# One more step of rest at three places of a two-layer attention and convolution trunk

## The chip, the core and the metric

The kernel runs on one core of one Trainium2 chip. The metric is the device time of one execution, in microseconds (us). Five engines work side by side, each through its own queue in order: TensorE (PE) does the matrix products, with its weight loads shown apart as PEld; VectorE (DVE) and ScalarE (ACT) work elementwise; GpSimd (POOL) does a little arithmetic and issues accumulating DMAs; SyncE (SP) issues the other DMAs. They wait for each other by semaphores.

## What is computed

Two layers run over 256 latent tokens of width 1024, with 256 context tokens beside them (512 columns in layer 0, 256 in layer 1, where only the latent tokens go on after the keys and values). The half of a layer that the change touches, cut to what matters:

```python
h = modulate(rmsnorm(x, norm1_g[l]), sh1, sc1)
p = h @ w_in[l]                                  # GLU, q, k, v, gates
u = dwconv1d(a * sigmoid(g), dw, dw_b)           # 31 taps, 512 channels
u = silu(layernorm(u, ln_g, ln_b))
y_conv = u @ w_conv_out[l]
y_attn = merge_heads(neighbourhood_attention(q, k, v, k_c, v_c, rpb)) @ w_na_out[l]
g_conv, g_attn = split(sigmoid(p[..., QKV_END:]))
x = x + g1 * ((g_conv * y_conv + g_attn * y_attn) @ w_out[l])
```

The second half of a layer is a gated MLP (2816 wide) with a convolution of width 3. A last RMSNorm gives the output. The modulation (shifts, scales and gates of both halves) is computed from a conditioning vector and six 1024 x 1024 matrices a layer.

## The kernel before

**Products.** Everything is float32. A weight tile is split into a high part `whi` and a low part `wlo`, an activation likewise, and each product is three matmuls: high by high (L197), high by low of the activation (L198), low of the weight by high (L199). A group is one block of 128 output channels: 8 tiles of weights, 24 matmuls, where the depth is 1024, and 4 tiles, 12 matmuls, where it is 512. The moving side has 512 columns in layer 0 and 256 in layer 1.

**Weights.** They come from memory in units of 512 KB (128 x 1024 floats) into a ring of four raw buffers; `whi` and `wlo` have four buffers each. A plain unit (`wunit`) is cast on ACT (L167), and DVE subtracts for the low part (L168). A unit in the set `ADDED` (`wadded`) goes another way: ACT casts (L216) and writes minus the high part (L217), and POOL issues a DMA that adds the raw unit onto it (L218). The cast into a `whi` buffer waits until PE has read what lay there, four units ago. In layer 0 the second and fourth unit of the attention's projection (NA) and all four of the convolution's projection (CO) are in `ADDED`.

**Side work.** Generators run beside the groups. `slot()` steps each of them once: after every group of 256 columns, and twice, in the middle and at the end, in a group of 512 columns. What a generator emits in a step lands in the program at that place; the scheduler that builds the program then sets each engine's order, by the data's ties and by its own estimate of the time. Such generators are: the attention's scores and values (`Attention.step`), the 31 taps of the convolution (L673), the modulation's dot products on DVE (`ada_dots`, L304, with rows `own` loaded by SP), and the layer norm of the convolution's branch.

**The layer norm** (`layer_norm`, L938) does, with yields between: the last taps; the sum over the four channel tiles (L951); a matmul with ones for the mean, L955, into the bank "po"; the subtraction of the mean (L958) and the sums of squares (squares L345 and L352 on ACT, sums L356 on DVE); the matmul that sums the squares, L370; the root on DVE and POOL (L378, L380); the transposes that spread it, L386; then for each tile j the scaling (L966), swish on ACT (L967), its high part `sh` (L968) and low part `sl` (L969). `last` is the second layer. After the gate groups come the eight NA groups (their result is multiplied onto a gate at L993 on DVE, which frees the bank), then the eight CO groups, which read `sh` and `sl`; their result is worked up at L998 to L1001 into `z`, named `h` in the trace, for the output projection.

**The attention** (`Attention.step`, L457): `n` counts steps, `at` is the step of its last action, `todo` holds pairs of heads with the step at which they came in.

Of the kernel before, what the change touches and what calls it, by code (L numbers as in the profile page):

```python
# [53 lines left out]
def trunk(ctx: ExitStack, tc: tile.TileContext, xt, cvec, crow, wall, wada, params, bias_t, rope_t, out):  # L54
# [13 lines left out]
    def nm(s):  # L68
        uid[0] += 1
        return f"{s}_{uid[0]}"  # L70
# [3 lines left out]
    def psum(tag="main"):  # L74
        return psp.tile([P, 512], F32, tag=tag, bufs=BANKS[tag], name=nm(tag))

    def tmp(w=512):
        return tp.tile([P, w], F32, tag="t", bufs=5, name=nm("t"))
# [67 lines left out]
    def pr(l, off, n):  # L146
        return par[:, l * NPAR + off : l * NPAR + off + n]
# [211 lines left out]
    def sum_squares(n, T, apart=False):  # L359

        at = tp.tile([P, 512], F32, tag="ss", name=nm("ss"))
        return [SumSq(T, at[:, i * T : (i + 1) * T], apart) for i in range(n)]

    def rstd(ss, n, bank, rest=0):

        nt = ss.T // P
        pt = psum("pt")
        for i, p in enumerate(ss.parts):
            for t in range(nt):
                pe.matmul(  # L370
                    pt[:, t : t + 1], sl(p, t), one, start=i == 0 and t == 0, stop=i == len(ss.parts) - 1,
                    skip_group_check=True,
                )
        return (yield from root(pt, nt, n, bank, rest))
# [48 lines left out]
    class Attention:  # L423
# [33 lines left out]
        def step(self, now=False):  # L457
            self.n += 1
            since = self.n - self.at
            alone = self.soft and not self.pv and not self.late  # L460
            rest = 4 if self.todo or alone else 3 if self.soft else 2
            if not now and since < (3 if alone and self.l else rest) and not self.late:
                return
            if not now and not alone and not self.todo and self.pairs < 4:
                return
            if not now and not alone and self.todo and self.n - self.todo[0][0] < 2:
                return
            if self.late:
                if not self.todo or self.n - self.todo[0][0] < 2:
                    return  # L470
                self.late, self.at = False, self.n
                return self.issue()
            if alone and not now:
                self.late = True
            self.at = self.n
            pv, self.pv = self.pv, []
            soft, self.soft = self.soft, []
            for what, its, pps in soft:
                with tc.issue_after(self.last.ins), tc.issue_after(self.done.ins):
                    self.turn(what, its, pps)  # L480
            for work in pv:
                self.values(*work, "sc" if work[0] == CTX and not (soft or self.todo) else "po")
            if self.todo and not self.late:
                self.issue()
# [147 lines left out]
    for l in range(DEPTH):  # L632
        last = l == DEPTH - 1
# [4 lines left out]
        with ExitStack() if last else start as e1a:  # L638
# [21 lines left out]
            def conv_tap(j, t):  # L660
                if after[0] is not None:
                    with tc.issue_after(after[0].ins):
                        tap(j, t)
                else:
                    tap(j, t)
# [259 lines left out]
            with ExitStack() as e1c:  # L925
# [12 lines left out]
                def layer_norm():  # L938

                    while taps:  # L940
                        for _ in range(6 if last else 5):
                            if taps:
                                conv_tap(*taps.pop(0))
                        yield
                    pace[0] = 1.0 if last else 1.2
                    flat = [c.rearrange("p s t -> p (s t)") for c in cb]
                    sm = tp.tile([P, 512], F32, tag="ss", name=nm("ss"))
                    eng = pool if last else dve
                    eng.tensor_tensor(sm[:, :T], flat[0], flat[1], ALU.add)
                    eng.tensor_tensor(sm[:, :T], sm[:, :T], flat[2], ALU.add)  # L950
                    dve.tensor_tensor(sm[:, :T], sm[:, :T], flat[3], ALU.add)  # L951
                    for _ in range(1 if last else 5):
                        yield
                    pm = psum("po")
                    pe.matmul(pm[:, :T], one.to_broadcast([P, P]), sm[:, :T], start=True, stop=True)  # L955
                    (s2,) = sum_squares(1, T)
                    for j in range(KC):
                        dve.scalar_tensor_tensor(flat[j], pm[:, :T], -1.0 / CONV, flat[j], ALU.mult, ALU.add)  # L958
                        s2.add(flat[j], j == KC - 1)
                    for _ in range(2 if last else 5):  # L960
                        yield
                    pb = yield from rstd(s2, CONV, "po", 0 if last else 2)
                    for j in range(KC):
                        sg = tmp()
                        g, b = pr(l, LNG + j, 1), pr(l, LNB + j, 1)
                        dve.scalar_tensor_tensor(flat[j], flat[j], g, pb[:, :T], ALU.mult, ALU.mult)  # L966
                        act.activation(sg[:, :T], flat[j], AF.Silu, bias=b)  # L967
                        act.copy(sh_[j], sg[:, :T])  # L968
                        dve.tensor_tensor(sl_[j], sg[:, :T], sh_[j].bitcast(F32), ALU.subtract)  # L969
                        yield  # L970
                    if last:
                        pace[0] = 0.4

                side.remove(conv)
                ln = layer_norm()
                add_side(ln)
                for n in range(n, 2 * KD):
# [356 lines left out]
```

## Time and profile before

| | us |
|---|---|
| median of 3 runs | 1056.72 (1055.75 to 1057.86) |
| the profiled execution, whole | 1057.85 |
| its span on the engines | 1056.0 |
| mean clock granted to TensorE | 0.996 of full speed |
| DVE busy in L168 | 252.5 (211 instructions) |
| DVE busy in L304 | 151.4 (120) |
| ACT busy in L167 | 217.6 (211) |

The page of the profile gives busy times by engine, groups of instructions by line, the chain of work that ended last, and DMA queues. A row of the timeline has the start, the duration, the engine, the line, the operation, output and inputs, and in brackets the idle time of its engine just before it and what ended that. PE rows overlap: matmuls are pipelined, so the pace is the distance of starts. DMA transfers are timed from issue to landing.

### The profile page before, as it was taken

Reading aid. Unit: us, or ns where it says so; the run is one execution under the profiler, and the core shown is the slowest. Engines: PE = TensorE matmul, PEld = TensorE weight load, DVE = VectorE, ACT = ScalarE, POOL = GpSimd, SP = SyncE. Lnnn points to the kernel's source line nnn. Section 1 sums busy time; section 2 is a strip of 40 time slices with the busy share of each in tenths; the row PEclk is TensorE's granted clock in tenths of the full one; section 3 lists DMA queues with packets and bytes.
Section 4 is the critical chain, followed back from the end, with each engine's and each line's share of the span. In section 5 each row is a group of like instructions: output and inputs, shape, how many; then the busy total and the mean of one; then the engine's idle time right before and its main releaser. Section 6 shows DMA issues by size and latency. Waiting matters only on the chain.

```text
span 1056.0 us, 18062 instructions
## 1 busy us (share of the span) xinstructions
PE 1033.4 (98%) x6886; PEld 933.1 (88%) x6886; DVE 892.1 (84%) x1630; ACT 568.1 (54%) x943; POOL 43.5 (4%) x59
## 2 busy tenths in 40 slices
PE   9999999999999999999999999999999999999997
PEld 7787788888889988888888889999889999999996
DVE  6568899999998788888889887799999988898883
ACT  4458868545434644444444223545776666667652
POOL 1111110011000000000000000000000000000000
PEclk9999999999999999999999999999999999999998
DMA  9988674888945345454545887556744484676781
GB/s 376 304 226 214 150 183 129 246 264 236 304 146 179 101 140 160 140 163 149 165 141 159 302 285 252 180 184 213 211 130 130 163 284 143 193 217 187 227 290 59
DMA packets 59511, 209.26 MB, mean 198 GB/s; under 512 B 7200, under 2 KB 7456, under 8 KB 59424
## 3 DMA queue, kind: packets, MB, share of 16 engines
q1 hardware_dynamic: 54384, 190.77, 55.6%
q0 software_dynamic: 4752, 17.30, 8.6%
q8 instruction: 54, 0.88, 0.3%
q14 instruction: 33, 0.27, 0.1%
q10 hardware_dynamic: 288, 0.04, 0.0%
HBM read 187.63 MB, written 1.05 MB: 179 GB/s over the span
## 4 chain that ended last, share of the span: by engine, by line
PE 68%; DVE 18%; ACT 5%; DMA 4%; issue 3%; SPq 1%; DVEq 0%; ACTq 0%
PE main L197 20%; PE main L198 20%; PE main L199 19%; DVE cb L673 6%; PE main L736 4%; DMA raw<-in_wall 3%; DVE wlo L168 2%; DVE t L304 2%; SPq L728 1%; PE sc L197 1%; PE sc L198 1%; PE sc L199 1%; ACT whi L167 1%; DVE qk L882 1%; PE po L230 1%
## 5 line engine op out<-in xcount | busy, mean ns | idle before, releaser
L197 PE MATMUL main<-h,whi 128*128 128x256 f32 (+1 forms) x1328 | 433.5, 327 | 1.9 <-DVE qk L882 1.2
L199 PE MATMUL main<-h,wlo 128*128 128x256 f32 (+1 forms) x1328 | 430.0, 325 | 3.0 <-DVE wlo L168 2.9
L198 PE MATMUL main<-h,whi 128*128 128x256 f32 (+1 forms) x1328 | 430.4, 325 | 0.9 <-DVE h L1001 0.7
L167 ACT CAST whi<-raw 128x1024 fp32r<-128x1024 f32 (+1 forms) x211 | 217.6, 1036 | 216.1 <-PE main L198 166.6
L168 DVE TENSOR_TENSOR wlo<-raw,whi 128x1024 fp32r<-128x1024 f32 (+1 forms) x211 | 252.5, 1203 | 66.4 <-ACT whi L167 66.0
L197 PEld LDWEIGHTS main<-h,whi 128*128 128x128 f32 x1328 | 253.0, 191 | 23.4 <-issue 1.7
L199 PEld LDWEIGHTS main<-h,wlo 128*128 128x128 f32 x1328 | 252.5, 191 | 20.6 <-DVE wlo L168 3.7
L198 PEld LDWEIGHTS main<-h,whi 128*128 128x128 f32 x1328 | 253.0, 191 | 18.3 <-DVE h L1001 1.0
L304 DVE CUSTOM_DVE_ANT_0 t<-own,sb,par 128x1024 bf16<-128x1024 f32 x120 | 151.4, 1277 | 7.2 <-DMA own<-in_wada 7.1
L673 DVE SCALAR_TENSOR_TENSOR cb<-u,par,cb 128x512 f32<-128x512 f32 (+1 forms) x240 | 144.1, 615 | 2.8
L198 PE MATMUL main<-fl,whi 128*128 128x256 f32 (+1 forms) x396 | 122.7, 310 | 0.0
L197 PE MATMUL main<-fh,whi 128*128 128x256 f32 (+1 forms) x396 | 122.7, 310 | 0.0
L199 PE MATMUL main<-fh,wlo 128*128 128x256 f32 (+1 forms) x396 | 122.6, 310 | 0.0
L198 PEld LDWEIGHTS main<-fl,whi 128*128 128x128 f32 x396 | 75.6, 191 | 3.6
L199 PEld LDWEIGHTS main<-fh,wlo 128*128 128x128 f32 x396 | 75.6, 191 | 3.5
L197 PEld LDWEIGHTS main<-fh,whi 128*128 128x128 f32 x396 | 75.6, 191 | 3.5
L216 ACT CAST whi<-raw 128x1024 fp32r<-128x1024 f32 x33 | 34.6, 1048 | 36.7 <-PE main L198 30.0
L1070 ACT ACTIVATE t<-main,par 128x512 f32<-128x512 f32 (+1 forms) x82 | 50.6, 666 | 0.7 <-PE main L199 0.7
L1071 DVE SCALAR_TENSOR_TENSOR t<-main,par,t 128x510 f32<-128x510 f32 (+1 forms) x82 | 47.3, 612 | 1.1 <-ACT t L1070 0.8
L1074 DVE SCALAR_TENSOR_TENSOR t<-main,par,t 128x510 f32<-128x510 f32 (+1 forms) x82 | 46.7, 609 | 0.0
L1083 ACT ACTIVATE t<-t 128x512 f32<-128x512 f32 (+1 forms) x44 | 23.1, 524 | 43.4 <-DVE t L1074 42.9
L404 ACT ACTIVATE h<-t,mod 128x256 fp32r<-128x256 f32 x56 | 25.2, 501 | 35.1 <-DVE t L403 34.7
(207 smaller groups left out, 1217.3 us busy)
## 6 DMA issues: line engine op xcount, KB each, us to landing
raw<-in_wall SPq DMA_DIRECT2D x240, 512.0 KB, 4.4
own<-in_wada SPq DMA_DIRECT2D x72, 512.0 KB, 4.7
wlo<-raw POOLq DMA_DIRECT2D x33, 512.0 KB, 5.5
raw<-in_wada SPq DMA_DIRECT2D x16, 512.0 KB, 5.9
bias<-in_bias_t SPq DMA_DIRECT2D x8, 520.0 KB, 5.1
row<-in_wada SPq DMA_DIRECT2D x8, 512.0 KB, 5.1
sb<-in_crow SPq DMA_DIRECT2D x5, 512.0 KB, 4.7
x<-in_xt SPq DMA_DIRECT2D x4, 512.0 KB, 5.0
```

Source lines behind the costliest of these rows:

```text
L167: act.copy(hi[:, c], r[:, c])
L168: dve.tensor_tensor(lo[:, c], r[:, c], hi[:, c].bitcast(F32), ALU.subtract)
L197: pe.matmul(ps, w[0], order(xh), start=start, stop=False)
L198: pe.matmul(ps, w[0], order(xl), start=False, stop=False)
L199: pe.matmul(ps, w[1], order(xh), start=False, stop=stop)
L216: act.copy(hi, r)
L304: dve.tensor_tensor_reduce(tmp().bitcast(BF16), r, v, 1.0, pr(l, BADA + n, 1), ALU.mult, ALU.add, mods[l][:, n, s : s + 1])
L673: dve.scalar_tensor_tensor(cb[j], src, w, cb[j], ALU.mult, ALU.add)
L736: mm = pe.matmul(pv[t], h1[n == 1][k][:, c], runs(w[n == 2][:, b]), start=k + n == 0, stop=k == KD - 1 and n == 2)
L1070: act.activation(c, pv_, AF.Identity, bias=pr(l, FDB + t, 1), scale=w[1])
L1071: dve.scalar_tensor_tensor(c[:, :, 1:], pv_[:, :, : S - 1], w[0], c[:, :, 1:], ALU.mult, ALU.add)
L1074: dve.scalar_tensor_tensor(c[:, :, : S - 1], pv_[:, :, 1:], w[2], c[:, :, : S - 1], ALU.mult, ALU.add)
```

## The change

Three numbers. The attention's first scores ask for three steps since the first pair came in instead of two, as long as no action has been taken (`at` is 0); layer 0's layer norm yields six times instead of five between the sum of the channel tiles and the mean's matmul; layer 1's yields three times instead of two between the sums of squares and the matmul that adds them up.

```diff
--- before.py
+++ after.py
@@ -463,7 +463,7 @@
                 return
             if not now and not alone and not self.todo and self.pairs < 4:
                 return
-            if not now and not alone and self.todo and self.n - self.todo[0][0] < 2:
+            if not now and not alone and self.todo and self.n - self.todo[0][0] < (2 if self.at else 3):
                 return
             if self.late:
                 if not self.todo or self.n - self.todo[0][0] < 2:
@@ -949,7 +949,7 @@
                     eng.tensor_tensor(sm[:, :T], flat[0], flat[1], ALU.add)
                     eng.tensor_tensor(sm[:, :T], sm[:, :T], flat[2], ALU.add)
                     dve.tensor_tensor(sm[:, :T], sm[:, :T], flat[3], ALU.add)
-                    for _ in range(1 if last else 5):
+                    for _ in range(1 if last else 6):
                         yield
                     pm = psum("po")
                     pe.matmul(pm[:, :T], one.to_broadcast([P, P]), sm[:, :T], start=True, stop=True)
@@ -957,7 +957,7 @@
                     for j in range(KC):
                         dve.scalar_tensor_tensor(flat[j], pm[:, :T], -1.0 / CONV, flat[j], ALU.mult, ALU.add)
                         s2.add(flat[j], j == KC - 1)
-                    for _ in range(2 if last else 5):
+                    for _ in range(3 if last else 5):
                         yield
                     pb = yield from rstd(s2, CONV, "po", 0 if last else 2)
                     for j in range(KC):
```

The first place leaves the order of instructions on every engine as it is. The others move instructions on PE, DVE and ACT, and on SP and POOL the loads and accumulates tied to them. In layer 0 L955, L370 and L386 stand 12 matmuls later on PE. DVE has two more of the modulation's dot products (L304) ahead of the sum L951.

First place, ACT in layer 0, from the cast of NA's fourth unit (`whi_2814`, low part `wlo_2815`) on; 2855 and 2904 are the casts of CO's first two units, and g_15 the last gate. Before:

```order
L216 CAST whi_2814<-raw_2812 128x1024
L711 ACTIVATE g_15_2667<-main_2614 128x512
L217 ACTIVATE wlo_2815<-whi_2814 128x1024
L967 ACTIVATE t_2662<-cb_3_187,par 128x512
L968 CAST sh_3_2152<-t_2662 128x512
L216 CAST whi_2855<-raw_2853 128x1024
L217 ACTIVATE wlo_2856<-whi_2855 128x1024
L216 CAST whi_2904<-raw_2902 128x1024
L217 ACTIVATE wlo_2905<-whi_2904 128x1024
```

After:

```order
L216 CAST whi_2814<-raw_2812 128x1024
L711 ACTIVATE g_15_2662<-main_2609 128x512
L967 ACTIVATE t_2657<-cb_2_186,par 128x512
L968 CAST sh_2_2151<-t_2657 128x512
L967 ACTIVATE t_2693<-cb_3_187,par 128x512
L968 CAST sh_3_2152<-t_2693 128x512
L216 CAST whi_2855<-raw_2853 128x1024
L216 CAST whi_2904<-raw_2902 128x1024
L217 ACTIVATE wlo_2815<-whi_2814 128x1024
L217 ACTIVATE wlo_2856<-whi_2855 128x1024
L217 ACTIVATE wlo_2905<-whi_2904 128x1024
```

The negated copy L217 into `wlo_2815` moved behind the swish of tiles 2 and 3 and behind the casts `whi_2855` and `whi_2904`.

Second place, DVE in layer 0, around the low part of NA's third unit, `wlo_2768`; g_8 to g_11 are the gates that NA's groups 0 to 3 are multiplied onto, `own` rows feed L304 (its second row reads out the accumulator). Before:

```order
L969 TENSOR_TENSOR sl_2_2155<-t_2639,sh_2_2151 128x512
L304 ISA t_2658,mod_105<-own_2583,sb_2146,par 128x1024
L304 ISA mod_105 128x1
L966 SCALAR_TENSOR_TENSOR cb_3_187<-cb_3_187,par,po_2585 128x512
L168 TENSOR_TENSOR wlo_2768<-raw_2766,whi_2767 128x1024
L304 ISA t_2712,mod_105<-own_2637,sb_2143,par 128x1024
L304 ISA mod_105 128x1
L969 TENSOR_TENSOR sl_3_2156<-t_2662,sh_3_2152 128x512
L993 SCALAR_TENSOR_TENSOR g_8_2328<-g_8_2328,main_2691 128x512
```

After:

```order
L993 SCALAR_TENSOR_TENSOR g_9_2367<-g_9_2367,main_2705 128x512
L304 ISA t_2745,mod_105<-own_2655,sb_2143,par 128x1024
L304 ISA mod_105 128x1
L304 ISA t_2747,mod_105<-own_2655,sb_2146,par 128x1024
L304 ISA mod_105 128x1
L993 SCALAR_TENSOR_TENSOR g_10_2430<-g_10_2430,main_2732 128x512
L993 SCALAR_TENSOR_TENSOR g_11_2469<-g_11_2469,main_2752 128x512
L168 TENSOR_TENSOR wlo_2768<-raw_2766,whi_2767 128x1024
L304 ISA t_2779,mod_105<-own_2716,sb_2143,par 128x1024
```

L168 of `wlo_2768` moved from ahead of the first L993 (g_8) to behind the fourth (g_11). On PE, the first two products of NA's groups 4 to 7 now stand ahead of the first product with `wlo_2768`.

Third place, ACT in layer 1, around the table load of L967 (swish); `whi_8687`, `whi_8729`, `whi_8771` are casts of three weight units in a row. Before:

```order
L167 CAST whi_8687<-raw_8686 128x1024
L967 ACT_TABLE_LOAD
L967 ACTIVATE t_8575<-cb_0_6566,par 128x256
L967 ACTIVATE t_8594<-cb_1_6567,par 128x256
L968 CAST sh_0_8285<-t_8575 128x256
L968 CAST sh_1_8286<-t_8594 128x256
L967 ACTIVATE t_8619<-cb_2_6568,par 128x256
L967 ACTIVATE t_8638<-cb_3_6569,par 128x256
L968 CAST sh_2_8287<-t_8619 128x256
L968 CAST sh_3_8288<-t_8638 128x256
L167 CAST whi_8729<-raw_8728 128x1024
L167 CAST whi_8771<-raw_8770 128x1024
```

After:

```order
L167 CAST whi_8687<-raw_8686 128x1024
L167 CAST whi_8729<-raw_8728 128x1024
L967 ACT_TABLE_LOAD
L967 ACTIVATE t_8589<-cb_0_6566,par 128x256
L967 ACTIVATE t_8614<-cb_1_6567,par 128x256
L968 CAST sh_0_8285<-t_8589 128x256
L968 CAST sh_1_8286<-t_8614 128x256
L967 ACTIVATE t_8633<-cb_2_6568,par 128x256
L967 ACTIVATE t_8639<-cb_3_6569,par 128x256
L968 CAST sh_2_8287<-t_8633 128x256
L968 CAST sh_3_8288<-t_8639 128x256
L167 CAST whi_8771<-raw_8770 128x1024
```

The cast `whi_8729` moved from behind the last L968 to ahead of the table load. On PE, L370 stands one matmul later and L386 twelve.

## The prediction

> **What bounds the kernel now.** I read the page first: busy times and the chain of the work that ended last.
>
> ```profile
> span 1056.0 us, 18062 instructions
> PE 1033.4 (98%) x6886; PEld 933.1 (88%) x6886; DVE 892.1 (84%) x1630; ACT 568.1 (54%) x943; POOL 43.5 (4%) x59
> ...
> PE 68%; DVE 18%; ACT 5%; DMA 4%; issue 3%; SPq 1%; DVEq 0%; ACTq 0%
> ```
>
> TensorE is busy for 1033.4 of 1056.0 us, so all its idle time, start and tail included, is 22.6 us. A change of order can gain only out of this idle time; it can lose as much as it lays bare. DVE at 84% is near enough to full to lay something bare. Next come the stretches that the change touches, by windows (columns: PE, weight load, DVE, ACT, POOL, granted clock, DMA share, GB/s), and the list of PE's waits.
>
> ```profile
> 236.00:292.00 56.00, 56.00 (x263) 49.04 (x262) 51.30 (x81) 27.63 (x34) 5.25 (x6) 1.00 0.91 265
> 292.00:330.00 38.00, 37.34 (x252) 34.14 (x251) 34.79 (x72) 13.43 (x24) 0.72 (x1) 1.00 0.41 131
> 812.00:846.00 34.00, 32.06 (x280) 31.39 (x279) 32.03 (x73) 21.16 (x43) 0.71 (x1) 1.00 0.51 163
> ...
> PE main L199 <- DVE wlo L168: 2.9, 3, 1.5
> PE sc L136 <- POOL ident masks.py:199: 1.8, 1, 1.8
> ```
>
> In layer 0 (236 to 292 us) PE has no idle time: nothing can be gained there, and DVE is 92% busy (51.30 of 56.00), DMA 91%. In layer 1 (812 to 846) PE is idle for 1.94 us. No wait of PE in the whole span is longer than 1.8 us. The clock granted is 1.00 in both.
>
> **Edit 1** (L466) is costed at nothing. Its line asks for 3 steps since the first pair of heads instead of 2, but two lines above, the attention already asks for 4 steps since its last action, and before the first action that count starts at zero, as the first pair's does at the earliest. The stricter test is always met already. If that reading is wrong, the price is one step of 12 matmuls later for one head pair, without a wait of PE for it to remove.
>
> **Edit 2** (L952, layer 0), at the mean's matmul. PE first, then DVE:
>
> ```profile
> 213.28 0.38 PE L199 MATMUL main<-h,wlo 128*128 128x512 f32 x1
> 213.96 1.12 PE L955 MATMUL po<-ss,one 128*128 128x512 f32 x2 [0.30 <-DVE ss L951]
> ...
> 239.12 0.60 PE L386 MATMUL po<-ident,rs 128*128 128x128 f32 x4
> ...
> 247.33 0.38 PE L197 MATMUL main<-oh,whi 128*128 128x512 f32 x1
> ...
> 257.26 0.38 PE L198 MATMUL main<-ol,whi 128*128 128x512 f32 x1
> ...
> 268.05 0.38 PE L197 MATMUL main<-sh,whi 128*128 128x512 f32 x1
> ```
> ```profile
> 213.21 0.69 DVE L951 TENSOR_TENSOR ss<-ss,cb 128x512 f32<-128x512 f32 x1
> ...
> 239.76 2.06 DVE L966 SCALAR_TENSOR_TENSOR cb<-cb,par,po 128x512 f32<-128x512 f32 x3 [2.45 <-PE po L386]
> ...
> 242.56 1.28 DVE L304 CUSTOM_DVE_ANT_0 t<-own,sb,par 128x1024 bf16<-128x1024 f32 x1
> ...
> 243.77 1.28 DVE L304 CUSTOM_DVE_ANT_0 t<-own,sb,par 128x1024 bf16<-128x1024 f32 x1
> ...
> 249.25 1.22 DVE L168 TENSOR_TENSOR wlo<-raw,whi 128x1024 fp32r<-128x1024 f32 x1
> ...
> 251.59 0.68 DVE L969 TENSOR_TENSOR sl<-t,sh 128x512 fp32r<-128x512 f32 x1
> 252.19 0.68 DVE L993 SCALAR_TENSOR_TENSOR g<-g,main 128x512 f32<-128x512 f32 x1
> ```
>
> From the first matmul of the attention projection (NA, 12 matmuls a group) to the 47th, 247.33 to 257.26, comes the pace: 46 steps in 9.93 us, 0.216 us a matmul, so one slot of 12 is 2.59 us. L955 would have started 0.22 after 213.28, at 213.50, and started at 213.96: 0.46 is lost. In the new order two L304 (1.21 us each, 242.56 to 243.77) stand ahead of the sum L951, which then ends about 213.9 + 2.4 = 216.3; PE arrives at 213.50 + 2.59 = 216.1. About 0.2 is still waited for, up to all of 0.46; I take **-0.3**, so NA's groups start at 247.0.
>
> L386 goes to 239.12 + 2.59 - 0.3 = 241.4, and L966 follows 0.64 behind (239.12 to 239.76): 242.05. DVE, which waited 2.45 us there, waits about five: it was given two L304 early, but nothing else to do. What then stands in one piece up to the low part of NA's third unit (L168 wlo_2768) is longer than before. Before: 239.76 to 249.25, 9.49 us. Now it has four L304 more (4.8), one L969 (0.6) and four L993 (0.6 each, 2.4): 17.3 us. So that L168 starts at 242.05 + 17.3 = 259.3 in place of 249.25 and ends at 260.5. PE is through with NA's fourth group at about 257.3 (247.0 plus 48 matmuls of 0.216), issues 8 high-part products that now stand ahead (1.7 us; the last two wait for L993 of groups 2 and 3 to free their banks), and waits for the L168: 257.3 + 1.7 = 259.0 to 260.5, **1.5 us** of stall that did not exist. Twenty matmuls, 4.3 us, lead to 264.8.
>
> There the next new wait stands. ACT and POOL of before:
>
> ```profile
> 247.32 1.04 ACT L216 CAST whi<-raw 128x1024 fp32r<-128x1024 f32 x1 [1.56 <-PE main L198]
> ...
> 248.76 1.06 ACT L217 ACTIVATE wlo<-whi 128x1024 fp32r<-128x1024 f32 x1
> ...
> 257.68 1.04 ACT L216 CAST whi<-raw 128x1024 fp32r<-128x1024 f32 x1 [3.05 <-PE main L198]
> ...
> 250.22 0.86 POOL L218 DMA_DIRECT2D wlo<-raw  x1 [9.89 <-PE main L199]
> ...
> DMA to landing us min/median/max: 5.5/8.0/10.6
> ```
>
> The low part of NA's fourth unit (wlo_2815) is made in three steps: cast, negated copy (L217, 248.76), accumulating DMA (L218, 250.22). In the new order the L217 stands behind the cast of whi_2904, whose buffer comes free with PE's last L198 of NA's fourth group (257.26; the cast ran 257.68 to 258.72). ACT runs in order, so the L217 slips from 248.76 to about 258.5, ten us, and the DMA from 250.22 to about 259.9. It lands 5.5, 8.0 or 10.6 us behind (minimum, median, maximum over this stretch): 265.4, 267.9 or 270.5. PE is there at 264.8. Twenty matmuls (4.3) then lead to the conv branch: 269.7, **272.2** or 274.8, against 268.05. I take the median, as the DMA share there is 0.91 and two further accumulates follow at its heels: term **+4.1**, from +1.0 (the DMA hides behind the L168's stall) to +6.8. The 0.3 gained is inside it. Behind it, the branch's own low parts (accumulated next, at about 261 and 262) land by 272 with the longest of those three times. One DMA of SP is moved too: the load that takes the raw buffer of the late unit waits for its accumulate.
>
> ```profile
> raw<-in_wall SPq DMA_DIRECT2D x240, 512.0 KB, 4.4
> ```
>
> From 267.9 it takes 4.4 us, then cast, copy and accumulate 1.0 + 1.0 + 8.0: ready at 282.3, wanted by the conv branch's seventh group at 272.2 + 6 x 2.59 = 287.7. That is covered by 5 us; without the cover its lateness would be added whole. The own rows queued behind it on SP feed only DVE's L304.
>
> A rule to weigh: PE's wait may cost more than its length. Every window here shows a granted clock of 1.00, and the longest wait was 1.8 us, so no row prices a longer one; twenty matmuls at half the pace would cost 4.3 us more, the upper end, and nothing the lower. The Trainium skill, "TensorE: Matmul & The Clock Gate", Part 1, says that after an idle window of about 3.4 us the array runs at half rate until another such window was busy. My wait of 267.9 - 264.8 = 3.1 us is just below; by that page a wait across a whole window would add some 1.7 us (estimate from its figure). No run here shows it yet.
>
> **Edit 3** (L960, layer 1).
>
> ```profile
> 823.01 0.61 PE L370 MATMUL pt<-one,ss 128*128 128x1 f32 x4 [0.96 <-DVE ss L356]
> ...
> 825.01 0.43 PE L386 MATMUL po<-ident,rs 128*128 128x128 f32 x2
> ...
> 826.05 0.28 PE L198 MATMUL main<-ol,whi 128*128 128x256 f32 x1
> 826.16 0.28 PE L199 MATMUL main<-oh,wlo 128*128 128x256 f32 x1
> ...
> 829.29 0.28 PE L197 MATMUL main<-sh,whi 128*128 128x256 f32 x1
> ...
> 841.73 0.38 PE L199 MATMUL main<-h,wlo 128*128 128x256 f32 x1 [0.88 <-DVE wlo L168]
> ```
> ```profile
> 823.19 1.28 ACT L967 ACT_TABLE_LOAD   x1
> 826.05 0.51 ACT L967 ACTIVATE t<-cb,par 128x256 f32<-128x256 f32 x1 [1.58 <-DVE cb L966]
> ...
> 827.19 0.69 ACT L968 CAST sh<-t 128x256 fp32r<-128x256 f32 x2
> ...
> 829.20 1.99 ACT L167 CAST whi<-raw 128x1024 fp32r<-128x1024 f32 x2
> ```
>
> The sums' matmul L370 moves by one matmul only, so of its wait of 0.96 just 0.11 goes (826.05 to 826.16 is one matmul): **-0.1**. L386 moves by 12 matmuls, 1.3 us, to about 826.2. On ACT the cast of whi_8729 (half of the 1.99 at 829.20) now stands ahead of the table load for L967. The cast needs PE's L198 of the same group as 826.05, which in the new order ends just ahead of L386: about 826.3 to 827.3. The load, hidden at 823.19 before, runs 827.4 to 828.7; the first L967 starts at 828.7 in place of 826.05, and its high part (1.14 later before, from 826.05 to the L968 at 827.19) at 829.9, the low part a DVE step later, 830.4. PE wants them at 829.29 - 0.1: **+1.1** of new stall. At 841.73 a wait of 0.88 for an L168 stands; the casts of the output projection's units come earlier in the new order, and I let it go: **-0.9**. The casts there now stand ahead of some of the L1000, whose high parts the projection waits for: **+0.3** (an L1000 is 0.4, behind a cast of 1.04, for a part of its time). Sum of the edit: **+0.4**; from -1.0 (no stall at 829, both other gains) to +2.0 (no gain at 841, and the cast of 1.04 in full).
>
> Whether the table load costs more than its 1.28 us, the row at 823.19 does not tell, since its user comes long after. An earlier one does:
>
> ```profile
> 82.57 1.28 ACT L519 ACT_TABLE_LOAD   x1
> 83.86 0.61 ACT L519 ACTIVATE pp<-sc,mx 128x416 f32<-128x416 f32 x1
> ```
>
> The user starts 1.29 behind the load. The Trainium skill, "ScalarE: Activation LUTs", What ACT_TABLE_LOAD costs, gives 1283 ns and a drain of about 1380 ns, 2.66 us a switch. The first figure agrees; a drain behind the load does not show here. By the page the stall at 829 would be 1.4 longer and the time 1062.6, inside the forecast's case, of which I give it one part in ten.
>
> **Sum.** 4.1 + 0.4 = +4.5 us: the profiled execution of 1057.85 us (span 1056.0 and 1.85 around it) would become 1062.3. The profile was 1.1 above the median, so against the median of 1056.72 I say **1061.2 us**.
>
> **The rivals.**
> - *The accumulate hides.* If it lands in 5.5 us or less, PE waits for the L168 alone: +1.0, with layer 1 between -1.0 and +0.9, so +0.0 to +1.9: about 1057.7. For it: the minimum row; against it: the median of 8.0.
> - *Faster: the feed of low parts.* One mechanism: PE's waits for sums and low parts (0.46 at L955, 0.96 at L370, 0.88 at 841.73) all go, and the stall at 259 does not come. Sum -2.3, about 1054.4. It decides so if ACT's L217 is not held by the cast (that is, if the whi buffer is free before PE leaves NA's fourth group). Against it: the cast's releaser at 257.68 is PE's L198.
> - *The edits do nothing.* Layer 0's loss is made good later, since PE, late by 4, finds weights and DVE's results already there. For it: the waits named in PE's list. Against it: from 292 to 330 PE is idle for 0.66 us in all (37.34 of 38.00), so 4.5 - 0.7 - 1.9 (that of 812 to 846) leaves +1.9: 1058.6.
> - *Late landing.* The DMA takes 10 us or more, as the maximum did: term +6.0 to +6.8, 1063.1 to 1063.9.
> - *Clock.* PE's wait near 265 is long enough for the granted clock to fall: up to 4.3 on top of the forecast, 1065.5. Against it: no fall in any window. The page above states the rule, and its estimate would give 1062.9.
>
> **How the numbers follow.** Forecast (landing near the median): 0.52; late landing 0.15; clock 0.05; hidden accumulate 0.11 and loss made good 0.10; faster 0.07. A measurement of this kernel tells 0.2%, 2.1 us, from no change. Slower by more is 0.72 (forecast, late landing and clock); within is 0.21; faster is 0.07. The range leaves out the faster case and little of the top: 1056.7 (+1.0 and layer 1 at -1.0) to 1065.5 (1056.72 + 6.8 + 2.0, nearly both upper ends).
>
> **What would show it.** Right: in the profile after, L217 of the fourth NA unit behind a second L216 near 258, L218 near 260 instead of 250.2, an L199 of PE near 260 waiting 1 to 2 us for L168, and one near 265 waiting about 3 us for the DMA of wlo; the conv branch starts near 272 rather than 268.05. In layer 1, the table load near 827 and a wait of PE near 829 for the high or low part of the conv branch. Wrong: PE still without idle time between 236 and 292, or those waits there and the span not longer. If attention's first scores stand elsewhere, edit 1 was misread.

## The result and the profile after

| | before | after |
|---|---|---|
| median, us | 1057.98 (6 runs, 1055.75 to 1059.60) | 1065.59 (6 runs, 1063.87 to 1068.68) |
| profiled execution / its span | 1057.85 / 1056.0 | 1065.13 / 1063.3 |

The changed kernel takes 1.0071 times the time of the one before, with a 95% interval of 1.0056 to 1.0086: 7.5 us slower. Foretold were 1061.2 us, 4.5 above a median of 1056.72; on that median the measured ratio gives 1064.2, within the stated 1056.7 to 1065.5. The direction held; the size was short by 3. The page after:

```profile
span 1063.3 us, 18058 instructions
PE 1038.1 (98%) x6886; PEld 935.5 (88%) x6886; DVE 892.9 (84%) x1630; ACT 568.1 (53%) x943; POOL 43.5 (4%) x59
```

The span grew by 7.3 us. PE has the same 6886 matmuls and is still "98% busy", but its busy time grew by 4.7 us (1033.4 to 1038.1) and its idle time by 2.6 (22.6 to 25.2). Equal work with more busy time means that matmuls ran slower or overlapped less. The windows say where (columns as before the change, the clock granted ahead of the DMA share):

```profile
236.00:292.00 56.00, 53.99 (x249) 46.12 (x248) 43.73 (x70) 24.83 (x31) 5.26 (x6) 1.00 0.82 236
292.00:330.00 38.00, 34.91 (x191) 29.70 (x190) 33.59 (x63) 11.68 (x20) 0.00 (x0) 0.91 0.43 130
```

From 236 to 292 us PE now has 2.0 us of idle time where it had none, and DVE's busy time in the same 56 us fell from 51.30 to 43.73. From 292 to 330 the clock is 0.91. PE's timeline, with the waits in brackets, shows the stages:

```profile
258.23 0.48 PE L197 MATMUL main<-oh,whi 128*128 128x512 f32 x1 [0.27 <-DVE g L993]
...
259.96 0.48 PE L199 MATMUL main<-oh,wlo 128*128 128x512 f32 x1 [0.44 <-DVE wlo L168]
...
265.85 0.48 PE L199 MATMUL main<-oh,wlo 128*128 128x512 f32 x1 [1.30 <-DMA wlo<-raw]
...
270.27 0.38 PE L197 MATMUL main<-sh,whi 128*128 128x512 f32 x1
...
294.83 0.48 PE L198 MATMUL main<-h,whi 128*128 128x512 f32 x1 [0.87 <-DVE h L1001]
...
296.09 0.48 PE L197 MATMUL main<-h,whi 128*128 128x512 f32 x1 [0.56 <-ACT h L1000]
297.83 0.79 PE L198 MATMUL main<-h,whi 128*128 128x512 f32 x1 [1.26 <-DVE h L1001]
...
300.25 0.80 PE L198 MATMUL main<-h,whi 128*128 128x512 f32 x1 [0.35 <-DVE h L1001]
```

The two new waits in NA are where the prediction put them: 259.96 for the low part from DVE, 265.85 for the accumulating DMA. The conv branch starts at 270.27, 2.2 us later than before (268.05): NA starts 0.75 us earlier (246.58 for 247.33) and takes 3.0 us longer. That is less than the +4.1 foretold. The rest comes where the prediction saw nothing: the output projection waits four times for `h`, the merged rows, 3.04 us in all. After it, the next norm's matmul with ones (L370, same instruction in both profiles) starts at 332.12 instead of 323.93. The last `h` (the last L1001 on DVE) comes at 303.72 instead of 297.43. Before, then after:

```profile
297.43 0.68 DVE L1001 SCALAR_TENSOR_TENSOR h<-t,h 128x512 fp32r<-128x512 f32 x1
...
323.93 0.61 PE L370 MATMUL pt<-one,ss 128*128 128x1 f32 x4
```
```profile
303.72 0.69 DVE L1001 SCALAR_TENSOR_TENSOR h<-t,h 128x512 fp32r<-128x512 f32 x1
...
332.12 0.60 PE L370 MATMUL pt<-one,ss 128*128 128x1 f32 x4
```

So of 8.2 us lost up to there, 2.2 are there when the conv branch starts, 4.1 more when the last `h` is ready (6.3 us late in all), and 1.9 come behind it: from the last L1001 to L370 are 28.4 us instead of 26.5. The last part falls where the clock is at half; more of it below. (The whole span grew by 7.3: 0.9 us come back later, where was not traced.) For the 4.1, ACT and DVE tell why. Before, ACT had the first two L1000 at:

```profile
272.47 0.63 ACT L1000 ACTIVATE h<-t 128x512 fp32r<-128x512 f32 x1 [2.30 <-DVE t L999]
...
275.18 0.63 ACT L1000 ACTIVATE h<-t 128x512 fp32r<-128x512 f32 x1 [0.92 <-DVE t L999]
```

After, ACT and DVE:

```profile
256.92 1.05 ACT L216 CAST whi<-raw 128x1024 fp32r<-128x1024 f32 x1 [3.60 <-PE main L198]
257.87 2.95 ACT L217 ACTIVATE wlo<-whi 128x1024 fp32r<-128x1024 f32 x3
266.07 1.05 ACT L216 CAST whi<-raw 128x1024 fp32r<-128x1024 f32 x1 [5.25 <-DMA raw<-in_wall]
...
274.35 1.05 ACT L216 CAST whi<-raw 128x1024 fp32r<-128x1024 f32 x1 [6.14 <-DMA raw<-in_wall]
...
276.39 0.61 ACT L1000 ACTIVATE h<-t 128x512 fp32r<-128x512 f32 x1
279.59 1.05 ACT L167 CAST whi<-raw 128x1024 fp32r<-128x1024 f32 x1 [2.58 <-DMA raw<-in_wall]
282.53 0.64 ACT L1000 ACTIVATE h<-t 128x512 fp32r<-128x512 f32 x1 [1.89 <-DVE t L999]
```
```profile
277.04 0.69 DVE L1001 SCALAR_TENSOR_TENSOR h<-t,h 128x512 fp32r<-128x512 f32 x1 [2.56 <-ACT h L1000]
...
280.67 1.22 DVE L168 TENSOR_TENSOR wlo<-raw,whi 128x1024 fp32r<-128x1024 f32 x1 [2.34 <-ACT whi L167]
```

ACT waits 6.14 us for a raw weight unit, and the first L1000 (at 272.47 before) stands behind that cast. Then the cast of the next unit waits 2.58 us, and on DVE its subtraction L168 stands ahead of L999 and waits 2.34. The second L1000 starts at 282.53, 7.4 us later than before (275.18). DVE is without a gap from 286 on, so these waits are not made good: the last L1001 starts at 303.72, 6.3 us after the one before (297.43).

### The profile page after: what moved, and what is told of

The parts are those of the page before. It is cut to its first block, busy times and chain, and to the rows that moved or that the text cites. A ratio compares the mean times of both kernels' runs of the same rounds, so it can differ in the third digit from the quotient of the medians.

```text
span 1063.3 us, 18058 instructions
## 1 busy us (share of the span) xinstructions
PE 1038.1 (98%) x6886; PEld 935.5 (88%) x6886; DVE 892.9 (84%) x1630; ACT 568.1 (53%) x943; POOL 43.5 (4%) x59
## 4 chain that ended last, share of the span: by engine, by line
PE 74%; DVE 12%; ACT 6%; issue 3%; DMA 3%; SPq 1%; DVEq 0%; ACTq 0%; POOLq 0%; POOL 0%
PE main L197 21%; PE main L198 21%; PE main L199 21%; PE main L736 4%; DVE cb L673 3%; DVE wlo L168 3%; DMA raw<-in_wall 2%; SPq L728 1%; ACT whi L167 1%; PE sc L197 1%; PE sc L199 1%; PE sc L198 1%; DMA wlo<-raw 1%; ACT whi L216 1%; PE po L230 1%
## 5 line engine op out<-in xcount | busy, mean ns | idle before, releaser
L168 DVE TENSOR_TENSOR wlo<-raw,whi 128x1024 fp32r<-128x1024 f32 (+1 forms) x211 | 253.3, 1207 | 68.8 <-ACT whi L167 68.2
L304 DVE CUSTOM_DVE_ANT_0 t<-own,sb,par 128x1024 bf16<-128x1024 f32 x120 | 151.8, 1282 | 5.6 <-DMA own<-in_wada 5.6
L216 ACT CAST whi<-raw 128x1024 fp32r<-128x1024 f32 x33 | 34.6, 1049 | 42.4 <-PE main L198 25.4
L404 ACT ACTIVATE h<-t,mod 128x256 fp32r<-128x256 f32 x56 | 25.2, 503 | 34.8 <-DVE t L403 34.6
```

The costliest lines, as they stand in the source:

```text
L168: dve.tensor_tensor(lo[:, c], r[:, c], hi[:, c].bitcast(F32), ALU.subtract)
L216: act.copy(hi, r)
L304: dve.tensor_tensor_reduce(tmp().bitcast(BF16), r, v, 1.0, pr(l, BADA + n, 1), ALU.mult, ALU.add, mods[l][:, n, s : s + 1])
```

## The experiments

Layer 0 and layer 1 apart, each with its own number alone:

```diff
-                    for _ in range(1 if last else 5):   # layer0_alone
+                    for _ in range(1 if last else 6):
```
```diff
-                    for _ in range(2 if last else 5):   # layer1_alone
+                    for _ in range(3 if last else 5):
```

> The second edit alone (six yields ahead of layer 0's mean). Theory A (all of the loss arises in layer 0: a late low part, then a late weight load that blocks ACT and DVE ahead of the output projection, then a lower clock): the time is 7 to 9 us above the kernel before, PE waits near 260 and 265 and again 3 us between 293 and 301, at a granted clock near half for some us. Rival B (layer 1's edit gives a part of the loss): at most +5 us here, the rest with the third edit.

> The third edit alone (three yields in layer 1). Theory A: between -1.5 and +0.5 us against the kernel before, with the table load behind a cast near 827 and a new wait near 829, made good at the waits behind it. Rival B: +2 us or more. If the first edit did anything, it would be missing here and in the run of the second edit alone, and the two would not add up to the whole change's +7.5 us.

Layer 0's edit alone gives 1.0077 (1.0064 to 1.0091), layer 1's alone 1.0000 (0.9988 to 1.0012). Within their intervals the two add up to the whole change (1.0071), so nothing is left over for the first edit, whose build orders every engine as before. Rival B falls. Layer 1's run shows the new wait on PE and its cause on ACT, the table load (1.28 us) behind a cast that PE holds up:

```profile
831.46 0.60 PE L197 MATMUL main<-sh,whi 128*128 128x256 f32 x3 [0.71 <-ACT sh L968]
```
```profile
827.82 1.07 ACT L167 CAST whi<-raw 128x1024 fp32r<-128x1024 f32 x1 [3.04 <-PE main L198]
828.91 1.28 ACT L967 ACT_TABLE_LOAD   x1
830.20 0.91 ACT L967 ACTIVATE t<-cb,par 128x256 f32<-128x256 f32 x2
```

The 0.71 is paid and the 0.88 that PE waited for an L168 at 841.73 before is not in this run: it comes out even, within 1.3 us.

**The order on ACT in NA.** The whole change, with the copy put back ahead of the casts:

```diff
-        act.copy(hi, r)
-        act.mul(lo, hi.bitcast(F32), -1.0)
+        with tc.issue_after(neg[0]) if l == 0 and U_NA <= u < U_WO else ExitStack():
+            act.copy(hi, r)
+        neg[0] = act.mul(lo, hi.bitcast(F32), -1.0).ins
```

> The whole change, with one tie more: in layer 0, each cast of a unit with accumulated low part (attention and convolution projections) goes behind the negated copy of the unit before it. On ACT two copies move ahead of two casts, nothing else. Theory A (that copy behind a cast that waits for PE is the root): the accumulate of the fourth unit starts near 254 in place of 259.3, the wait near 265 and the 3 us near 295 are gone, the clock stays at 1.00, and 5 to 7 us of the 7.5 come back (+0.5 to +2.5 against before). Rival C (the loss comes from DVE, whose low part of the third unit went behind four gate products): the wait for DVE near 260 stays and with it +4 us or more.

Two L217 move ahead of two L216 on ACT, and no other engine's order changes. The time is 1.0017 (1.0008 to 1.0027) of the kernel before: 5.7 of the 7.5 us come back. Timeline of ACT, POOL, PE and DVE in that run:

```profile
252.40 1.05 ACT L217 ACTIVATE wlo<-whi 128x1024 fp32r<-128x1024 f32 x1
```
```profile
253.87 0.86 POOL L218 DMA_DIRECT2D wlo<-raw  x1 [14.16 <-ACT wlo L217]
```
```profile
260.08 0.48 PE L199 MATMUL main<-oh,wlo 128*128 128x512 f32 x1 [0.43 <-DVE wlo L168]
```
```profile
299.25 0.68 DVE L1001 SCALAR_TENSOR_TENSOR h<-t,h 128x512 fp32r<-128x512 f32 x1
```

The accumulate starts 5.5 us earlier (253.87 for 259.34) and PE's wait for it is gone. DVE's L168 still holds PE for 0.43 us: rival C is right that this wait stays, and wrong that most of the loss is in it. About 1.8 us against the kernel before are left, whose cause was not tested. The last L1001 is 4.5 us earlier than with the whole change, and the clock stays at 1.00. PE's waits for `h` do not vanish, as was expected, but shrink from 3.04 us to 1.42 (0.20, 0.56 and 0.66); the run with layer 1's edit alone, whose layer 0 is that of before, has as much.

**What stands behind the late load.** The whole change, with the cast of the output projection's first unit behind the fourth L1000:

```diff
-            act.copy(hi[:, c], r[:, c])
+            with tc.issue_after(hs[3]) if (l, u) == (0, U_WO) else ExitStack(): act.copy(hi[:, c], r[:, c])
...
-                    act.mul(z[0][n][:, :T], t, 0.5)
+                    hs.append(act.mul(z[0][n][:, :T], t, 0.5).ins)
```

> The whole change, with one tie more: the cast of the output projection's first weight unit goes behind the fourth L1000 of layer 0. Theory A's second half (the late load of that unit holds up ACT and, by its subtraction, DVE, and so the rows h that the output projection waits for): the waits for h near 293 to 300 shrink from 3.0 us to under 1 and the clock stays at 1.00, so the time is 4 to 6 us below that of the whole change, while the waits near 260 and 265 stay. Rival D (h is late because its projection itself started 2.2 us later, and DVE's dot products fill the rest): the waits for h stay at 2 us or more, and the time is within 2 us of the whole change's.

The time is 1.0028 (1.0018 to 1.0038): 4.5 of the 7.5 us come back, though the accumulate is as late as ever. PE in that run:

```profile
266.33 0.48 PE L199 MATMUL main<-oh,wlo 128*128 128x512 f32 x1 [1.23 <-DMA wlo<-raw]
...
295.64 0.48 PE L198 MATMUL main<-h,whi 128*128 128x512 f32 x1 [0.55 <-DVE h L1001]
296.91 0.48 PE L197 MATMUL main<-h,whi 128*128 128x512 f32 x1 [0.56 <-ACT h L1000]
298.05 0.48 PE L198 MATMUL main<-h,whi 128*128 128x512 f32 x1 [0.66 <-DVE h L1001]
```

The waits for `h` fell from 3.04 us to 1.77, not to "under 1" as expected, and the clock stayed at 1.00. The last L1001 starts 2.2 us earlier than with the whole change (301.52 for 303.72), and L370 follows it by 26.6 us instead of 28.4. The tie also moved some work on DVE and a load on SP, so the 4.5 us are not the one cast's price to the tenth. But the mechanism shows: a cast and a subtraction that wait for a load hold up what stands behind them.

**The clock.** The whole change, with twelve matmuls put where PE waits for `h`:

```diff
+            for _ in range(4 if fill is not None and k > 4 else 0): pe.matmul(fill[:, c], ws[0][0], runs(xh[0][:, c]), start=True, stop=True)
...
-                    ps = group(psum(), unit8(l, U_WO + n), *z, ALL)
+                    ps = group(psum(), unit8(l, U_WO + n), *z, ALL, psum("sc") if l + n == 0 else None)
```

> The whole change, with twelve matmuls more in the first group of layer 0's output projection: four each ahead of its sixth, seventh and eighth part, where PE waits for h; they write a bank that nothing reads. Theory E (the waits of 3.0 us leave PE so idle that the granted clock falls to half for some 7 us, and that is about half of the loss there): the twelve, 2.6 us at the full pace, fit into the waits, PE is busy, the clock stays at 1.00, and the time is 2 to 3.5 us below the whole change's, though PE does more. Rival F (the clock falls for another reason, or its fall hides in the waits for h): the time is equal or up to 2.6 us above the whole change's.

The windows after the whole change, and then with the filling:

```profile
294.00:296.00 2.00, 0.70 (x2) 0.30 (x2) 2.00 (x5) 0.59 (x2) 0.00 (x0) 1.00 0.68 246
296.00:298.00 2.00, 0.65 (x2) 0.35 (x3) 2.00 (x4) 0.97 (x2) 0.00 (x0) 0.95 0.49 180
298.00:300.00 2.00, 1.85 (x3) 0.62 (x3) 2.00 (x4) 0.63 (x1) 0.00 (x0) 0.50 0.00 0
```
```profile
298.00:300.00 2.00, 1.18 (x5) 1.05 (x6) 2.00 (x5) 0.59 (x1) 0.00 (x0) 1.00 0.17 68
300.00:302.00 2.00, 1.37 (x7) 0.88 (x6) 2.00 (x5) 0.04 (x1) 0.00 (x0) 1.00 0.19 31
```

The filling kept the clock at 1.00, so too little work on PE is what lowered it. But the time is 1.0077 (1.0055 to 1.0099), no better than the whole change. That does not make the fall free, because the filling also changed PE's order. In the whole change, twelve products of the next group stand ahead of the first product with the last `h`; in the filled program they stand behind it. That product after the whole change, and then with the filling:

```profile
305.52 0.59 PE L197 MATMUL main<-h,whi 128*128 128x512 f32 x2
```
```profile
304.30 0.70 PE L197 MATMUL main<-h,whi 128*128 128x512 f32 x2 [1.50 <-ACT h L1000]
```

With the filling PE waits 1.50 us for the last L1000, with the twelve (2.6 us at the full pace) still to do. In the whole change that `h` was ready at 303.26 (L1000 at 302.63, 0.63 long), and PE came to it 2.3 us later, since most of the twelve ran at half the pace.

The distance from the last L1001 to L370 gives an estimate of the price. It is 26.5 us before and with layer 1's edit alone, and 26.4 and 26.6 in the last two experiments; in all four the clock stayed at 1.00 there. It is 28.4 in the whole change and 29.0 with layer 0's edit alone, where the clock fell. With the filling it is 28.9 at full clock: about the twelve products more than 26.4. So the fall costs about 1.9 us of the 8.2. Theory E's mechanism holds, and this price is at the low end of what it gave; but no run changes the clock alone, so the price is worked out and not shown.

**The table load** in layer 1: the third edit alone, with the cast behind the last swish.

```diff
-            act.copy(hi[:, c], r[:, c])
+            with tc.issue_after(sw[-1]) if (l, u) == (1, U_CO + 2) else ExitStack(): act.copy(hi[:, c], r[:, c])
...
-                        act.activation(sg[:, :T], flat[j], AF.Silu, bias=b)
+                        sw.append(act.activation(sg[:, :T], flat[j], AF.Silu, bias=b).ins)
```

> The third edit alone, with one tie more: in layer 1 the cast of CO's third unit (whi_8729) goes behind the last swish L967, so the table load stands where it stood before. Theory G (the load behind that cast makes PE's wait of 0.71 us for sh near 831): the wait is 0.2 us or less, and the wait for a low part early in the output projection (0.88 us before) comes back; the time is within 1 us of the kernel before. Rival H (sh is late because its root and transposes are one group later): a wait of 0.5 us or more for sh stays.

The time is 0.9998 (0.9981 to 1.0015). No wait for `sh` is left, and the old wait is back:

```profile
841.95 0.38 PE L199 MATMUL main<-h,wlo 128*128 128x256 f32 x1 [0.59 <-DVE wlo L168]
```

Theory G holds: the earlier cast buys the low part in the output projection with the table load.

**The opposite move**: the kernel before, with one yield less in layer 0.

```diff
-                    for _ in range(2 if last else 5):
+                    for _ in range(2 if last else 4):
```

> The kernel before, with one yield less between layer 0's sums of squares and the matmul that adds them up (four for five), so the transposes stand one step earlier: the opposite move. Theory I (in this stretch DVE's idle time is what the sum is paid in; the wait of 2.45 us in front of L966 is idle time that this step can fill): DVE waits there under 1 us, its last L1001 ahead of the output projection ends 0.5 to 2 us earlier than at 298.1, PE's wait of 0.66 us for h near 294 is gone, and the time is 0.3 to 1.2 us below the kernel before. Rival J (the wait in front of L966 is slack, since PE is full to 292): DVE waits elsewhere instead, for PE's groups, and the time is the same within 0.3 us.

The time is 0.9994 (0.9984 to 1.0004), no difference that can be told. PE's wait for `h` near 294 stays (0.66 us, with another of 0.52 ahead of it), and DVE still waits in front of L966, and for rows of the modulation later:

```profile
293.65 0.48 PE L198 MATMUL main<-h,whi 128*128 128x512 f32 x1 [0.66 <-DVE h L1001]
```
```profile
236.33 2.06 DVE L966 SCALAR_TENSOR_TENSOR cb<-cb,par,po 128x512 f32<-128x512 f32 x3 [2.94 <-PE po L386]
...
267.04 1.28 DVE L304 CUSTOM_DVE_ANT_0 t<-own,sb,par 128x1024 bf16<-128x1024 f32 x1 [1.55 <-DMA own<-in_wada]
```

The last L1001 starts at 297.13, 0.3 us earlier than before, where L955 was already 0.8 earlier (213.12 for 213.96). So every sign of theory I failed: the work just moved up, and DVE waited as long, only earlier. No version here beats the kernel before beyond its interval.

## Why the prediction held, and where it was short

- **Edit 1 at nothing**: the program is the same, and the other two add up without it.
- **The mean's wait, -0.3**: not settled. L955 waits for nothing in the profile after (215.79), but 0.64 us in the run of layer 0 alone, against 0.30 before.
- **DVE's low part, 1.5 us of stall**: right. The wait is at 259.96, foretold near 260. The idle times of 0.27 and 0.44 leave out the lost overlap; by the distance of starts, as the prediction counts, the product at 259.96 is 1.3 us late (five starts of 0.216 behind 257.58). DVE's long piece came out within 0.6 us (L966 was foretold for 242.05, the L168 for 259.3; it started at 258.69):

```profile
241.60 1.41 DVE L966 SCALAR_TENSOR_TENSOR cb<-cb,par,po 128x512 f32<-128x512 f32 x2 [5.75 <-PE po L386]
```

- **The copy behind the cast**: right, and shown by putting it back. L217 foretold for 258.5, measured 257.87; the DMA for 259.9, measured 259.34:

```profile
259.34 2.76 POOL L218 DMA_DIRECT2D wlo<-raw  x3 [19.76 <-ACT wlo L217]
```

  It let PE go on at 265.85, 6.5 us after the issue, where the median of 8.0 was taken. By the distance of starts PE lost 1.5 us there, where 3.1 were foretold. So the term of +4.1 is +2.2.
- **The step that failed** is the one on SP's load: "covered by 5 us". It asked when PE wants the late unit, and not what stands behind that unit's cast on ACT, where the order is the same before and after, so that no row of the difference showed it. It followed one load only, and not the next unit's, which waits for the second of the late accumulates. (A third one, behind the late L168, also moved, from 250.54 to 259.98.) SP's queue, before and after, shows the next unit's load (L164) go out 8.2 us later:

```profile
260.54 0.33 SPq L164 DMA_DIRECT2D raw<-in_wall  x1
```
```profile
265.86 0.33 SPq L154 DMA_DIRECT2D raw<-in_wall  x1
...
268.78 0.67 SPq L164 DMA_DIRECT2D raw<-in_wall  x1
```

  And it priced a load at 4.4 us, the median of the whole run, in a stretch where DMA was 91% busy. The two that count, issued at 265.86 and 268.78, let their casts start at 274.35 and 279.59: 8.5 and 10.8 us. The DMA view of the kernel before, from 250 to 268, had a price for such a stretch (KB each, median us to landing):

```profile
raw<-in_wall SPq DMA_DIRECT2D x3, 512.0 KB, 7.5
```

  What came of it: the first L1000 is 1.7 us, the second 5.1 us later than the 2.2 us by which the conv branch moved (276.39 and 282.53, against 272.47 and 275.18 before). In the end the last `h` comes 4.1 us later than that, and the clock adds about 1.9: two terms that the sum did not have.
- **Edit 3, +0.4**: measured 0.0 with an interval of 1.3 us to either side. The wait for `sh` is 0.71 (foretold 1.1), the wait at 841.73 went as foretold. The first L967 starts 1.29 us after its table load here too (830.20 behind 828.91). The Trainium skill, "ScalarE: Activation LUTs", What ACT_TABLE_LOAD costs, has a drain of about 1380 ns besides the load: no run here shows it.
- **The rivals.** The hidden accumulate, the faster case and the loss made good fell: the loss grew behind NA. So did the late landing: the time is near its 1063.1 to 1063.9, but the DMA took 6.5 us and not 10. The clock fell, but at other waits than the one named, and for about 1.9 us, not 4.3. The sentence that no window showed a fall held for the windows that were read; the last section has one from the kernel before.
- **Luck.** Of the 4.5 us foretold, 2.2 came where they were placed. That the sum still came within 3 us of the measured 7.5 is partly chance: terms that were too large (the landing, edit 3) made up for some of the two that were missing.

## What to carry to other kernels

When a load or a low part comes later, look past the engine that reads it: list what stands behind the instruction that waits for it on each in-order engine, also where the order has not changed. Price a DMA by the stretch it runs in and not by the median of the run. And a step of rest that takes a wait of a few tenths from the main engine can turn the order of other engines far behind it, so read the built order before the number. That holds for experiments too: matmuls added to fill a wait moved twelve others behind it.

## What was not expected of the hardware

In the changed kernel the granted clock fell to 0.50 near 298 us, though none of PE's waits there was longer than 1.26 us. In the four us before, PE was busy for 1.35 (0.70 and 0.65 in the windows above), and the matmuls came 0.43 us apart from 300.83 to 304.25, about twice the 0.216 of full pace. With the filling, PE was busy for 2.17 of 4 us at its least (1.37 in the window from 300 and 0.80 in the next), and the clock stayed at 1.00:

```profile
302.00:304.00 2.00, 0.80 (x4) 0.37 (x2) 2.00 (x4) 0.38 (x1) 0.00 (x0) 1.00 0.64 231
```

The Trainium skill, "TensorE: Matmul & The Clock Gate", Part 1, ties the lower rate to an idle window of about 3.4 us. No window here was idle throughout.

It is not the only fall. The clock of the kernel before fell near 98 us, behind a wait of 1.65 us, and in the profile after it also fell near 130, behind one of 1.69. The windows of before and after:

```profile
98.00:100.00 2.00, 1.91 (x11) 1.40 (x11) 1.93 (x4) 0.96 (x1) 0.63 (x1) 0.58 0.99 231
```
```profile
130.00:132.00 2.00, 2.00 (x10) 1.40 (x8) 1.96 (x5) 0.53 (x2) 0.00 (x0) 0.64 0.94 258
```

In the four us ahead of these two PE was busy for 1.86 and 2.27. So a third busy was not enough to keep the clock, and about a half sometimes was and sometimes was not; what decides between the two stays open.
